# Linear attention on one core: K and V in 8 KB rows over eight heads, K's features written twice, a first matmul 128 wide

## The chip, the cores and the metric

The kernel runs on one core of a Trainium2 chip. A core has five engines with an instruction queue each: TensorE (PE, matrix products; PEld is its loading of weights), VectorE (DVE), ScalarE (ACT), GpSimd (POOL) and SyncE (SP). Each engine takes its instructions in the order in which the program gives them, and waits where one needs a result of another engine. Sixteen DMA engines move data between the chip's memory (DRAM) and the on-chip memory (SBUF, 128 partitions); POOL and SP issue the transfers here. PE writes to a second on-chip memory, PSUM, of eight banks. The metric is the device time of one execution in microseconds (us); lower is better.

## The reference

For every batch and head (8 x 12 of them, 512 rows of 64 elements, all f32) the kernel computes attention without a softmax, by way of a 64 x 64 matrix per head:

```python
Q_feat = np.maximum(0, Q) + 1
K_feat = np.maximum(0, K) + 1
KV = np.einsum('bhkd,bhkv->bhdv', K_feat, V)
K_sum = np.sum(K_feat, axis=2)
numerator = np.einsum('bhqd,bhdv->bhqv', Q_feat, KV)
denominator = np.einsum('bhqd,bhd->bhq', Q_feat, K_sum)
return numerator / (denominator[:, :, :, None] + 1e-10)
```

## The kernel before

The 49,152 rows of Q, K and V are cut into 6 steps of 16 heads. One transfer loads 2 MB of one input and writes it as 1 MB of bf16 (the cast is done on the way, by transfers that POOL issues); a step needs one each of K, V and Q. The output leaves as f32 in 12 transfers of 1 MB.

A **group** g (12 of them, two to a step) has eight heads. K and V lie in rows of 16 x 64 elements to a partition (4 KB in DRAM, `C2 = 16`), so a head fills 32 partitions, and four heads share a tile; a group takes two such tiles, n = 0 and 1. Q lies in rows of 32 x 64 elements (8 KB), so a head of Q fills 16 partitions.

For each group the program has these parts:

- `k_features` (L141): two DVE instructions of 1024 elements (L137) compute max(K + 1, 1), the same as max(0, K) + 1, for n = 0 and 1 into `kf`.
- `v_blocks` (L148): V is copied into `v_all`, a constant tile whose 32-partition blocks are a block diagonal: block b of the partitions fills columns 64b to 64b + 63 of 256, the rest stays zero, and 4 more columns hold ones for the sum over K's features. Three of the four blocks are copied by DVE (L155), one by ACT (L153). `clear` (L237) writes the zeros and ones once, at the start.
- `keys_values` (L166): the first product. For 16 values of c and n = 0, 1 a matmul with K's features as weights (128 partitions, 64 columns) and `v_all` as the moving operand (260 columns). The matmuls for n = 0 write PSUM partitions 0 to 63, those for n = 1 write 64 to 127. Four casts by ACT (L181, L182) put the result into `kva_diag`, as blocks on a diagonal.
- `q_features` (L159) and `transposes` (L184): Q's features by DVE, then 16 transposes on PE into two banks and two copies by ACT (L195) into `qt`.
- `output`: `out_matmuls` (L197), the second product, 32 matmuls with `qt` as weights (64 columns) and 130 moving columns; and `norms` (L214), four times a reciprocal of the denominator (L222) and a multiply (L223) from PSUM into `o_sb`, on DVE. A product of 8 matmuls fills two banks, and there are two such pairs, so PE runs at most two ahead of the norms.
- `load`, `load_q` and `store` (L96, L110, L122) issue the transfers. All loads but the first K, and all stores but the last two groups', are issued by POOL in one queue. `in_pool` has two buffers for each of K, V and Q, so the loads of step s + 2 wait for the copies of step s.

The order on each engine is written out by hand (`manual_schedule`, L247 on). A group's turn is: K's features, V copies, then `output` of the group two before, then transposes or Q features, then `keys_values` of this group. So on PE the output matmuls of an earlier group stand ahead of this group's first product. The last two groups have an order of their own (L282 to L299).

Of the kernel before, what the change touches and what calls it, by code (L numbers as in the profile page):

```python
# [9 lines left out]
BF16 = mybir.dt.bfloat16  # L10
ALU = mybir.AluOpType

BANK = 512
IN_BUFS = 2
OUT_BUFS = 3
LAG = 3
# [3 lines left out]
def kernel(  # L20
# [10 lines left out]

# [4 lines left out]
    C = 8  # L44
    C2 = 2 * C
    C4 = 4 * C
    R = 4
    NPAIR = B * H * S // (P * C)
    NP = 4
    NG = NPAIR // NP  # L50
# [5 lines left out]

    q_eights = view(Q, C4)
    k_dram = view(K, C2)
    v_dram = view(V, C2)
# [3 lines left out]
    head_pool = ctx.enter_context(tc.tile_pool(name="head_pool", bufs=1))  # L63
    in_pool = ctx.enter_context(tc.tile_pool(name="in_pool", bufs=IN_BUFS))
    kf_pool = ctx.enter_context(tc.tile_pool(name="kf_pool", bufs=2))
    qf_pool = ctx.enter_context(tc.tile_pool(name="qf_pool", bufs=3))
# [8 lines left out]
    NV = 4  # L75
    v_all = const.tile([P, 2, 2, C2, 4 * D1], BF16, name="v_all")
    ones = const.tile([P, 4], BF16, name="ones")
    zero = const.tile([P, 1], FP32, name="zero")
    kva_all = const.tile([P, NV, 4, 2, D1], BF16, name="kva_all")
    kva_diag = [kva_all[:, i] for i in range(NV)]  # L80

    drams = dict(k=k_dram, v=v_dram)
    raw = {}
    bufs = {}
# [4 lines left out]
    cells_of = {}  # L89

    def load_first_k():
        k_raw = head_pool.tile([P, 2, C2, D], FP32, name="k_first")
        nc.sync.dma_start(out=k_raw, in_=k_dram[:, 0:4:2])
        raw["k", 0] = k_raw

    def load(x, groups):  # L96
        s = groups[0] // 2
        if groups[0] % 2 == 0 or (x, s) not in bufs:
            bufs[x, s] = in_pool.tile([P, 4, C2, D], BF16, name=f"{x}_raw")
        if len(groups) == 2:  # L100
            ms = slice(0, 4)
            of = slice(4 * s, 4 * s + 4)
        else:
            ms = slice(groups[0] % 2, 4, 2)
            of = slice(4 * s + groups[0] % 2, 4 * s + 4, 2)
        nc.gpsimd.dma_start(out=bufs[x, s][:, ms], in_=drams[x][:, of])  # L106
        for g in groups:
            raw[x, g] = bufs[x, s][:, g % 2 : 4 : 2]

    def load_q(s):  # L110
        t = in_pool.tile([P, 2, C4, D], BF16, name="q_raw")
        nc.gpsimd.dma_start(out=t, in_=q_eights[:, 2 * s : 2 * s + 2])  # L112
        rows = t.rearrange("p n (r c) d -> p n r c d", c=C)
        for e in range(2):
            raw["q", 2 * s + e] = rows[:, :, :, 4 * e : 4 * e + 4]

    def load_pair(s):
        load("k", (2 * s, 2 * s + 1))
        load("v", (2 * s, 2 * s + 1))
        load_q(s)  # L120

    def store(g):  # L122
        s = g // 2
        o_to = o_dram[:, 2 * NP * s : 2 * NP * s + 2 * NP]
        if g < NG - 2:
            nc.gpsimd.dma_start(out=o_to[:, g % 2 : 2 * NP : 2], in_=outs[s][:, g % 2 : 2 * NP : 2])  # L126
            return
        if g == NG - 2:
            nc.sync.dma_start(out=o_to[:, 0 : 2 * NP : 2], in_=outs[s][:, 0 : 2 * NP : 2])
            return  # L130
        for h in range(2):
            nc.sync.dma_start(
                out=o_to[:, 2 * h + g % 2 : 2 * NP : NP], in_=outs[s][:, 2 * h + g % 2 : 2 * NP : NP]
            )

    def feature(dst, src):
        nc.vector.tensor_scalar(  # L137
            out=dst, in0=src, scalar1=1.0, scalar2=1.0, op0=ALU.add, op1=ALU.max
        )

    def k_features(g):  # L141
        k_raw = raw.pop(("k", g))
        kf = kf_pool.tile([P, C2, 2, D], BF16, name="kf")
        for n in range(2):
            feature(kf[:, :, n], k_raw[:, n])
        kfs[g] = kf

    def v_blocks(g):  # L148
        v_raw = raw.pop(("v", g))
        for b in range(4):  # L150
            ps = slice(32 * b, 32 * b + 32)
            if b == 3:
                nc.scalar.copy(out=v_all[ps, g % 2, :, :, b * D : b * D + D], in_=v_raw[ps])  # L153
            else:
                nc.vector.tensor_copy(  # L155
                    out=v_all[ps, g % 2, :, :, b * D : b * D + D], in_=v_raw[ps]
                )

    def q_features(g):  # L159
        q_raw = raw.pop(("q", g))  # L160
        qf = qf_pool.tile([P, R, C // 2, 2, D], BF16, name="qf")
        for n in range(2):
            feature(qf[:, :, :, n], q_raw[:, n])
        qfs[g] = qf

    def keys_values(g):  # L166
        kf = kfs.pop(g)
        kva_ps = psum_kva.tile([P, 4 * D1], FP32, name="kva_ps")
        for c in range(C2):
            for n in range(2):  # L170
                nc.tensor.matmul(  # L171
                    kva_ps[64 * n : 64 * n + 64],
                    lhsT=kf[:, c, n, :],
                    rhs=v_all[:, g % 2, n, c, :],
                    start=(c == 0),
                    stop=(c == C2 - 1),
                )
        kva = kva_diag[g % NV]
        for n in range(2):
            ps = slice(64 * n, 64 * n + 64)  # L180
            nc.scalar.copy(out=kva[ps, :, n, 0:D], in_=kva_ps[ps, 0 : 4 * D].rearrange("p (b d) -> p b d", b=4))  # L181
            nc.scalar.copy(out=kva[ps, :, n, D], in_=kva_ps[ps, 4 * D : 4 * D1])  # L182

    def transposes(g):  # L184
        qf = qfs.pop(g)
        if g % 2 == 0:
            qts[g // 2] = mid_pool.tile([P, C, P, R], BF16, name="qt")
        for half in range(2):
            qt_ps = psum_qt.tile([P, 2, R, P], BF16, name="qt_ps")
            for c in range(2):  # L190
                for r in range(R):
                    nc.tensor.transpose(qt_ps[:, c, r], qf[:, r, 2 * half + c, :, :], identity)  # L192
            copy = nc.vector.tensor_copy if half and g == NG - 2 else nc.scalar.copy
            lo = g % 2 * 4 + 2 * half
            copy(out=qts[g // 2][:, lo : lo + 2], in_=qt_ps.rearrange("p c r q -> p c q r"))  # L195

    def out_matmuls(g, h):  # L197
        qt = qts[g // 2]
        kva = kva_diag[(g // 2 * 2 + h) % NV]
        ops = [psum.tile([P, 2, BANK], FP32, tag="ps", name="o_ps") for _ in range(2)]  # L200
        for c in range(C):
            for j in range(2):
                b = 2 * (g % 2) + j
                q = 16 * (4 * h + b)
                nc.tensor.matmul(  # L205
                    ops[c // 4][64 * j : 64 * j + 64, c // 2 % 2, (c % 2) * W : (c % 2) * W + W],
                    lhsT=qt[:, c, q : q + 16, :],
                    rhs=kva[:, b],
                    start=True,
                    stop=True,  # L210
                )
        cells_of[g, h] = ops

    def norms(g, h):  # L214
        ops = cells_of.pop((g, h))
        if (g % 2, h) == (0, 0):
            outs[g // 2] = out_pool.tile([P, 2 * NP, C, D], FP32, name="o_sb")
        o_sb = outs[g // 2]
        for i in range(2):
            cells = ops[i][:, :, 0 : 2 * W].rearrange("p b (c n x) -> p b c n x", n=2, x=D1)  # L220
            recip = recip_pool.tile([P, 2, 2, 2, 1], FP32, name="recip")
            nc.vector.reciprocal(out=recip, in_=cells[:, :, :, :, D:D1])  # L222
            nc.vector.tensor_tensor(  # L223
                out=o_sb[:, 2 * h + g % 2 : 2 * NP : NP, 4 * i : 4 * i + 4].rearrange(
                    "p n (b c) d -> p b c n d", b=2
                ),
                in0=cells[:, :, :, :, 0:D],
                in1=recip.to_broadcast([P, 2, 2, 2, D]),
                op=ALU.mult,
            )  # L230

    def output(g):
        for h in range(2):
            out_matmuls(g, h)
            norms(g, h)

    def clear(i):  # L237
        t = v_all[:, i].rearrange("p n c x -> p (n c x)").bitcast(FP32)
        w = t.shape[1] * 5 // 8
        nc.vector.memset(t[:, 0:w], 0.0)  # L240
        nc.scalar.copy(out=t[:, w:], in_=zero.to_broadcast([P, t.shape[1] - w]))  # L241
        nc.vector.tensor_copy(
            out=v_all[:, i, :, :, 4 * D : 4 * D1].rearrange("p n c j -> p (n c) j"),
            in_=ones[:, None, :].to_broadcast([P, 2 * C2, 4]),
        )

    with tc.manual_schedule():  # L247
        nc.vector.memset(zero, 0.0)
        load_first_k()
        load("v", (0,))  # L250
        load_q(0)
        load("k", (1,))
        load("v", (1,))
# [11 lines left out]
        for g in range(last - 1):  # L265
            if g % 2:
                transposes(g - 1)
# [64 lines left out]
```

## Time and profile before

| | |
|---|---|
| median of 3 runs | 126.66 us (126.54 to 127.17) |
| span of the profiled execution, first to last instruction | 124.7 us |
| mean granted clock of TensorE | 0.847 of full |
| read from and written to DRAM | 37.75 MB and 12.58 MB, 404 GB/s over the span |
| shares of the chain that ended last | DMA 56%, DVE 19%, PE 8%, ACT 6% |
| DMA from issue to landing, median of 1 MB loads of K, V, Q | 22.1, 23.0, 26.0 us |

The profile is one execution, recorded by the hardware. Busy time is the time in which an engine had an instruction running; an engine's idle time is put down to what ended it (the releaser, behind the arrow <-). The chain that ended last is followed back from the last instruction, at each step to what released it. GB/s count what is written, so a load that turns f32 into bf16 counts half of what it reads. From issue to landing a load takes four to five times as long as its own share of the traffic, since other transfers stand ahead of it in the queue.

### The profile page before, as it was taken

How to read it: one execution, taken by the hardware profiler on the slowest of the kernel's cores; microseconds unless marked ns; L12 is line 12 of the kernel's file. 1: busy time of each engine (PE TensorE's matmuls, PEld its weight loads, DVE VectorE, ACT ScalarE, POOL GpSimd, SP SyncE). 2: the span in 40 equal slices, each digit the busy share in tenths (PEclk: the TensorE clock that was granted, in tenths of full speed). 3: DMA queues.
4: the chain of work that ended last, by engine and by line, in shares of the span. 5: the costliest groups of instructions: out<-in, count | busy, mean ns of one | idle time of the engine just before them, and what ended most of it. 6: DMA issues, size and time to landing. Idle time of an engine off the chain costs nothing.

```text
span 124.7 us, 2348 instructions
## 1 busy us (share of the span) xinstructions
PE 61.8 (50%) x960; PEld 50.7 (41%) x960; DVE 89.3 (72%) x191; ACT 59.6 (48%) x86; POOL 26.1 (21%) x51
## 2 busy tenths in 40 slices
PE   0004945200692838539684691069495267775300
PEld 0003735200581827428573490058384155663100
DVE  4895444206999899997999930699959699969700
ACT  7532289306039781956639462601993295450000
POOL 6991023100011630233302420302020200020000
PEclk9999999955589999995999689756999958997555
DMA  3999999999999999999999999999999999999993
GB/s 95 330 214 214 209 198 210 210 214 213 208 213 213 216 214 208 212 213 217 230 405 327 210 212 214 215 338 403 227 212 215 218 255 415 420 413 416 406 409 126
DMA packets 11803, 32.13 MB, mean 258 GB/s; under 512 B 528, under 2 KB 528, under 8 KB 11792
## 3 DMA queue, kind: packets, MB, share of 16 engines
q0 software_dynamic: 10448, 28.84, 97.4%
q1 hardware_dynamic: 1344, 3.15, 6.7%
q8 instruction: 7, 0.11, 0.3%
q14 instruction: 4, 0.03, 0.1%
HBM read 37.75 MB, written 12.58 MB: 404 GB/s over the span
## 4 chain that ended last, share of the span: by engine, by line
DMA 56%; DVE 19%; PE 8%; ACT 6%; issue 3%; POOL 2%; POOLq 0%
DMA v_raw<-in_V_dram 30%; DMA q_raw<-in_Q_dram 26%; DVE o_sb L223 8%; PE kva_ps L171 5%; DVE v_all L155 5%; ACT v_all L153 3%; DVE qf L137 2%; PE qt_ps L192 2%; DVE recip L222 2%; ACT qt L195 2%; POOL v_raw L106 1%; DVE qt L195 1%; ACT kva_all L181 1%; POOL k_raw L106 1%; DVE kf L137 1%
## 5 line engine op out<-in xcount | busy, mean ns | idle before, releaser
L205 PE MATMUL o_ps<-kva_all,qt 128*64 128x130 bf16 x384 | 20.0, 240 | 37.0 <-DVE recip L222 27.0
L171 PE MATMUL kva_ps<-v_all,kf 128*64 128x260 bf16 x384 | 29.8, 320 | 15.8 <-DVE v_all L155 15.6
L155 DVE COPY v_all<-v_raw 32x2048 bf16<-32x2048 bf16 x36 | 25.8, 717 | 13.5 <-DMA v_raw<-in_V_dram 13.1
L223 DVE TENSOR_TENSOR o_sb<-o_ps,recip 128x512 f32<-128x512 f32 x48 | 33.2, 692 | 1.6
L171 PEld LDWEIGHTS <-kf 128*64 128x64 bf16 x384 | 24.6, 130 | 19.0 <-DVE v_all L155 16.0
L205 PEld LDWEIGHTS <-qt 128*64 128x64 bf16 x384 | 14.0, 118 | 42.2 <-issue 26.0
L153 ACT COPY v_all<-v_raw 32x2048 bf16<-32x2048 bf16 x12 | 22.6, 1893 | 16.9 <-DMA v_raw<-in_V_dram 16.7
L195 ACT COPY qt<-qt_ps 128x1024 bf16<-128x1024 bf16 x23 | 22.2, 1015 | 6.8 <-PE qt_ps L192 6.5
L181 ACT CAST kva_all<-kva_ps 64x256 bf16<-64x256 f32 x24 | 8.9, 371 | 27.5 <-PE kva_ps L171 27.3
L126 POOL DMA_DIRECT2D out_dram<-o_sb x10 | 8.6, 864 | 35.9 <-DVE o_sb L223 27.2
L192 PE MATMUL qt_ps<-identity,qf 128*128 128x128 bf16 x192 | 14.8, 235 | 2.0 <-ACT qt L195 1.3
L192 PEld LDWEIGHTS <-qf 128*128 128x128 bf16 x192 | 12.4, 106 | 4.5 <-issue 2.5
L137 DVE TENSOR_SCALAR kf<-k_raw 128x1024 bf16<-128x1024 bf16 x22 | 8.5, 426 | 7.6 <-DMA k_raw<-in_K_dram 7.6
L106 POOL DMA_DIRECT2D k_raw<-in_K_dram x6 | 4.9, 822 | 35.0 <-DVE kf L137 35.0
L222 DVE RECIPROCAL recip<-o_ps 128x8 f32<-128x8 f32 x48 | 9.6, 200 | 1.4 <-PE o_ps L205 1.2
L137 DVE TENSOR_SCALAR qf<-q_raw 128x1024 bf16<-128x1024 bf16 x24 | 8.8, 431 | 2.1 <-DMA q_raw<-in_Q_dram 2.0
L106 POOL DMA_DIRECT2D v_raw<-in_V_dram x7 | 5.4, 766 | 13.4 <-ACT v_all L153 9.3
L240 DVE MEMSET v_all<- 128x2600 f32 x2 | 4.5, 2225 | 0.9 <-issue 0.9
L112 POOL DMA_DIRECT2D q_raw<-in_Q_dram x6 | 4.3, 716 | 0.0
L182 ACT CAST kva_all<-kva_ps 64x4 bf16<-64x4 f32 x24 | 4.1, 170 | 0.0
L241 ACT COPY v_all<-zero 128x1560 f32<-128x1560 f32 x2 | 2.9, 1487 | 0.0
L261 POOL MEMSET kva_all<- 128x130 bf16 x16 | 2.4, 201 | 0.0
(13 smaller groups left out, 5.8 us busy)
## 6 DMA issues: line engine op xcount, KB each, us to landing
out_dram<-o_sb POOLq DMA_DIRECT2D x10, 1024.0 KB, 25.7
q_raw<-in_Q_dram POOLq DMA_DIRECT2D x6, 1024.0 KB, 26.0
k_raw<-in_K_dram POOLq DMA_DIRECT2D x5, 1024.0 KB, 22.1
v_raw<-in_V_dram POOLq DMA_DIRECT2D x5, 1024.0 KB, 23.0
k_first<-in_K_dram SPq DMA_DIRECT2D x1, 1024.0 KB, 4.9
v_raw<-in_V_dram POOLq DMA_DIRECT2D x2, 512.0 KB, 10.7
out_dram<-o_sb SPq DMA_DIRECT2D x1, 1024.0 KB, 7.0
out_dram<-o_sb SPq DMA_DIRECT2D x2, 512.0 KB, 6.4
```

The costliest lines, as they stand in the source:

```text
L106: nc.gpsimd.dma_start(out=bufs[x, s][:, ms], in_=drams[x][:, of])
L126: nc.gpsimd.dma_start(out=o_to[:, g % 2 : 2 * NP : 2], in_=outs[s][:, g % 2 : 2 * NP : 2])
L137: nc.vector.tensor_scalar(out=dst, in0=src, scalar1=1.0, scalar2=1.0, op0=ALU.add, op1=ALU.max)
L153: nc.scalar.copy(out=v_all[ps, g % 2, :, :, b * D : b * D + D], in_=v_raw[ps])
L155: nc.vector.tensor_copy(out=v_all[ps, g % 2, :, :, b * D : b * D + D], in_=v_raw[ps])
L171: nc.tensor.matmul(kva_ps[64 * n : 64 * n + 64], lhsT=kf[:, c, n, :], rhs=v_all[:, g % 2, n, c, :], start=(c == 0), stop=(c == C2 - 1),)
L181: nc.scalar.copy(out=kva[ps, :, n, 0:D], in_=kva_ps[ps, 0 : 4 * D].rearrange("p (b d) -> p b d", b=4))
L192: nc.tensor.transpose(qt_ps[:, c, r], qf[:, r, 2 * half + c, :, :], identity)
L195: copy(out=qts[g // 2][:, lo : lo + 2], in_=qt_ps.rearrange("p c r q -> p c q r"))
L205: nc.tensor.matmul(ops[c // 4][64 * j : 64 * j + 64, c // 2 % 2, (c % 2) * W : (c % 2) * W + W], lhsT=qt[:, c, q : q + 16, :], rhs=kva[:, ...
L222: nc.vector.reciprocal(out=recip, in_=cells[:, :, :, :, D:D1])
L223: nc.vector.tensor_tensor(out=o_sb[:, 2 * h + g % 2 : 2 * NP : NP, 4 * i : 4 * i + 4].rearrange("p n (b c) d -> p b c n d", b=2), in0=cell ...
```

## The change

K and V are now loaded in rows of 32 x 64 elements (8 KB), as Q is. A head fills 16 partitions, a tile holds eight heads, and a step s (`NPAIR` = 6) has two tiles, n = 0 and 1, each the work of one group before.

With two heads in each block of 32 partitions, the block diagonal of V alone no longer keeps them apart. K's features are therefore written twice, for a = 0 and 1, with the partitions of the other head at zero: instead of the constants 1 and 1 the instruction takes two values per partition from memory, `shift` and `least`, that make either max(K + 1, 1) or max(K + lowest, 0) = 0. `masks` computes them once, from bit 4 of the partition number. The two versions lie beside each other in `kf`, so that the first product is one matmul with 128 columns of weights per c, 32 of them per tile, in place of 2 x 16 with 64.

The stores write the same rows as before (2 KB), 12 of 1 MB; the last is no longer cut in two. `o_sb` is now six tiles of 1 MB in place of three of 2 MB, and the first K is loaded into one of them.

The order by hand is another one: in each half of a step `keys_values` now comes ahead of `output` of the step before, the transposes of a step stand at its end, and the last steps have no order of their own. The diff, cut to its core:

```diff
-    C2 = 2 * C
+    ROWS = 32
-    q_eights = view(Q, C4)
-    k_dram = view(K, C2)
-    v_dram = view(V, C2)
+    q_dram = view(Q, ROWS)
+    k_dram = view(K, ROWS)
+    v_dram = view(V, ROWS)
...
+    lane = const.tile([P, 1], I32, name="lane")
+    odd = const.tile([P, 1], I32, name="odd")
+    least = const.tile([P, 2], FP32, name="least")
+    shift = const.tile([P, 2], FP32, name="shift")
+    v_alls = [const.tile([P, ROWS, 4 * D1], BF16, name=f"v_all{i}") for i in range(2)]
+    kvas = [const.tile([P, 8, 2, D1], BF16, name=f"kva{i}") for i in range(2)]
...
+    def k_features(s, n):
+        k_raw = raw.pop(("k", s, n))
+        kf = kf_pool.tile([P, ROWS, 2, D], BF16, name="kf")
+        for a in range(2):
+            nc.vector.tensor_scalar(
+                out=kf[:, :, a],
+                in0=k_raw,
+                scalar1=shift[:, a : a + 1],
+                scalar2=least[:, a : a + 1],
+                op0=ALU.add,
+                op1=ALU.max,
             )
...
-        for c in range(C2):
-            for n in range(2):
-                nc.tensor.matmul(
-                    kva_ps[64 * n : 64 * n + 64],
-                    lhsT=kf[:, c, n, :],
-                    rhs=v_all[:, g % 2, n, c, :],
-                    start=(c == 0),
-                    stop=(c == C2 - 1),
-                )
+        for c in range(ROWS):
+            nc.tensor.matmul(
+                kva_ps,
+                lhsT=kf[:, c].rearrange("p a d -> p (a d)"),
+                rhs=v_alls[n][:, c],
+                start=(c == 0),
+                stop=(c == ROWS - 1),
+            )
+        kva = kvas[s % 2]
+        po = slice(64 * n, 64 * n + 64)
+        for a in range(2):
+            pi = slice(64 * a, 64 * a + 64)
+            nc.scalar.copy(
+                out=kva[po, a::2, n, 0:D],
+                in_=kva_ps[pi, 0 : 4 * D].rearrange("p (b d) -> p b d", b=4),
+            )
+            nc.scalar.copy(out=kva[po, a::2, n, D], in_=kva_ps[pi, 4 * D :])
...
+    def masks():
+        nc.vector.tensor_scalar(out=odd, in0=lane, scalar1=16, scalar2=None, op0=ALU.bitwise_and)
+        nc.vector.tensor_scalar(
+            out=least[:, 0:1], in0=odd, scalar1=-1.0 / 16, scalar2=1.0, op0=ALU.mult, op1=ALU.add
+        )
+        nc.vector.tensor_scalar(
+            out=least[:, 1:2], in0=odd, scalar1=1.0 / 16, scalar2=None, op0=ALU.mult
+        )
+        nc.vector.tensor_scalar(
+            out=shift, in0=least, scalar1=-1.0, scalar2=-LOWEST, op0=ALU.add, op1=ALU.mult
+        )
+        nc.vector.tensor_tensor(out=shift, in0=shift, in1=least, op=ALU.add)
...
+        nc.gpsimd.iota(lane, pattern=[[0, 1]], base=0, channel_multiplier=1)
...
         clear(0)
+        masks()
...
+        for s in range(NPAIR):
+            k_features(s, 0)
+            v_blocks(s, 0)
+            keys_values(s, 0)
+            if s:
+                output(s - 1, 0)
+                if s > 1:
+                    store(s - 2, 1, nc.gpsimd)
+            k_features(s, 1)
+            v_blocks(s, 1)
+            q_features(s)
+            keys_values(s, 1)
+            if s:
+                output(s - 1, 1)
+            if s + 2 < NPAIR:
+                load_k(s + 2)
+                load_v(s + 2)
+                load_q(s + 2)
+            if s:
+                store(s - 1, 0, nc.gpsimd)
+            transposes(s, 0)
+            transposes(s, 1)
+        s = NPAIR - 1
+        store(s - 1, 1, nc.gpsimd)
+        output(s, 0)
+        store(s, 0, nc.sync)
+        output(s, 1)
+        store(s, 1, nc.sync)
```

## The prediction

> **What bounds the kernel now.** I read the page first: which engine is busy when. Columns of its first line are busy us, share of the span and instructions; the strips cut the span into 40 slices, busy share in tenths and GB/s moved.
>
> ```profile
> PE 61.8 (50%) x960; PEld 50.7 (41%) x960; DVE 89.3 (72%) x191; ACT 59.6 (48%) x86; POOL 26.1 (21%) x51
> ...
> DMA  3999999999999999999999999999999999999993
> GB/s 95 330 214 214 209 198 210 210 214 213 208 213 213 216 214 208 212 213 217 230 405 327 210 212 214 215 338 403 227 212 215 218 255 415 420 413 416 406 409 126
> ...
> q0 software_dynamic: 10448, 28.84, 97.4%
> ```
>
> The 16 DMA engines are full from the second slice to the last, whatever computes. A load writes bf16 at about 213 GB/s (1.049 MB in 4.9 us), a store f32 at about 415 (1.049 MB in 2.5 us). Eighteen loads' worth (the first K in f32 at 2.5 us, the rest 85.8 us) and 12 stores (30 us) make 118 us of a 124.7 us span. The kernel is bound by DMA; no engine's own work reaches 90 us.
>
> Second, the groups by line with shapes kept apart, for prices (last columns: busy us, mean ns of one; idle us before the group and what ended it).
>
> ```profile
> L223 DVE TENSOR_TENSOR o_sb<-o_ps,recip 128x512 f32<-128x512 f32 x48 | 33.2, 692 | 1.6
> L171 PE MATMUL kva_ps<-v_all,kf 128*64 128x260 bf16 x384 | 29.8, 320 | 15.8 <-DVE v_all L155 15.6 <-ACT v_all L153 0.2
> L155 DVE COPY v_all<-v_raw 32x2048 bf16<-32x2048 bf16 x36 | 25.8, 717 | 13.5 <-DMA v_raw<-in_V_dram 13.1
> ...
> L153 ACT COPY v_all<-v_raw 32x2048 bf16<-32x2048 bf16 x12 | 22.6, 1893 | 16.9 <-DMA v_raw<-in_V_dram 16.7
> L195 ACT COPY qt<-qt_ps 128x1024 bf16<-128x1024 bf16 x23 | 22.2, 1015 | 6.8 <-PE qt_ps L192 6.5
> ...
> L137 DVE TENSOR_SCALAR kf<-k_raw 128x1024 bf16<-128x1024 bf16 x22 | 8.5, 426 | 7.6 <-DMA k_raw<-in_K_dram 7.6
> ...
> L137 DVE TENSOR_SCALAR kf<-k_first 128x1024 bf16<-128x1024 f32 x2 | 1.5, 782 | 0.0
> ```
>
> VectorE (DVE) waits for almost nothing but DMA. That is due to the order on PE: ahead of each step's first product stand the output matmuls of two steps before, whose inputs are long ready, so the norms follow the V copies without a wait.
>
> Third, the timeline (start, us taken by the run of instructions, engine, line), for runs of matmuls:
>
> ```profile
> 48.04 1.96 PE L171 MATMUL kva_ps<-v_all,kf 128*64 128x260 bf16 x32
> ...
> 50.14 1.07 PE L192 MATMUL qt_ps<-identity,qf 128*128 128x128 bf16 x16
> ...
> 51.14 0.64 PE L205 MATMUL o_ps<-kva_all,qt 128*64 128x130 bf16 x16
> ...
> 100.97 3.24 PE L171 MATMUL kva_ps<-v_all,kf 128*64 128x260 bf16 x32 [2.69 <-DVE v_all L155]
> ...
> 107.92 1.93 ACT L195 COPY qt<-qt_ps 128x1024 bf16<-128x1024 bf16 x2 [1.69 <-PE qt_ps L192]
> ...
> 108.58 1.98 PE L171 MATMUL kva_ps<-v_all,kf 128*64 128x260 bf16 x32
> ...
> 110.83 0.21 DVE L222 RECIPROCAL recip<-o_ps 128x8 f32<-128x8 f32 x1 [1.16 <-PE o_ps L205]
> ```
>
> A product (32 matmuls of the first kind) takes 1.98 us at its best (62 ns each) and more after an idle PE: 3.24 at 100.97, 3.68 for the run at 11.12, where the clock is low. The twelve sum to 29.8 us, 2.48 each. The last line shows what the change will make the rule: DVE waiting while a product ahead of its output matmuls runs.
>
> **The change part by part.** Nothing changes in number or shape for V copies (48), Q features (24), transposes (192), output matmuls (384), norms (48 reciprocals, 48 multiplies), casts of the product (48) and stores (12 MB). What changes:
>
> *Rows of 8 KB.* The end-of-transfer packets of the trace lie 4.89 to 4.92 us apart for the Q loads, whose rows are 8 KB already, and 4.95 to 5.60 for the ten 1 MB loads of K and V, 51.2 us in sum. All at 4.90 saves 2.2 us, at the least row 0.5. It counts only while DMA is the bound.
>
> *K's features twice.* 24 instructions stay 24, of 2048 elements in place of 1024, with a scalar from memory in place of constants. No row has such a scalar. Lower bound: the bf16 copy of 2048 elements, 0.69 us from one start to the next, 1.38 a pair (now 0.76). Upper: the multiply with two inputs, 512 in 0.692 us, so 5.5 a pair. I take 1.38, since operation, element type and output pitch are those of line 137, which at 1024 runs at about the copy's rate. The first pair reads f32: 1.48 us for 2 x 1024, so about 2.8 for 2 x 2048. A page bears on this: the Trainium skill, "PSUM — Partial Sum Buffer", section "Specifications (TRN2)", says that a [P, 1] operand passed as a scalar does not count among the inputs that decide whether VectorE takes two elements at a time; by that the pair is 1.38 and the first rival below falls, but no row here shows it.
>
> *Masks.* Five small DVE operations behind the first clear, between the 0.06 us of a small memset and the 0.20 of a reciprocal: 0.3 to 1.0, I take 0.6. Their iota on POOL (0.1 to 0.3, as its memset and select rows) stands behind four load issues and is done by about 4.6, when the clear is. First K features so start at 8.1, not 7.4.
>
> *First matmul 128 wide.* As many instructions (384), but the two 64-wide ones for two heads, which used separate halves of the array, become one over the whole array. Lower bound: 1.98 us a product, if width costs nothing. Upper: twice the slowest row, 7.4. Near rows: 16 transposes, 128 wide, 128 columns, take 1.07 us (67 ns); 16 output matmuls, 64 wide, 130 columns, 0.64 (40 ns). Halves of the array do run side by side, so I double: 3.96 at full clock, 4.97 at the mean (2 x 2.48), and 5.7 for the first, cold one (3.7 us of warming at twice 115 ns, the rest at 124). PE will have idle stretches of 3 to 5 us ahead of every product, so I take 4.97 for all others. A rule: the Trainium skill, "TensorE: Matmul & The Clock Gate", section "Back-to-back issue gap", gives 260/2.4 + 2.5 = 111 ns warm and 217 cold, so 3.55 and 6.9 us a product; all warm the sum below would be an estimated 159 us, and started cold for the 3.4 us that its section "What's actually happening" names, 5.2 each and 178.
>
> *The order, which decides.* On PE the product of a step now stands ahead of the output matmuls of the step before, and DVE has norms next behind the V copies. So DVE stands still through each product from the second step on, 10 times. Behind the waiting reciprocal wait the next K features and V copies, and for those the next product waits. Transposes stand at a step's end, their four copies on ACT ahead of ACT's share of the next V.
>
> One step, from the start of the four norms of an output's second half (0):
> - norms 3.45 (0.84 apart), K pair 1.38, V copies 2.15: DVE done at 6.98.
> - PE: last output matmuls at 2.1 (bank freed by the second norm), transposes 0.55 per 8; ACT's four copies (0.97 each, two banks) end at 6.5, ACT's V copy 1.89: 8.4.
> - product 8.5 to 13.4, first 8 output matmuls 0.27: norms at 13.7, then K pair and V copies: 20.7.
> - product again (Q features, 1.43, hidden in it) and 0.27: 26.0.
>
> A step is 26.0 us, where DMA needs 14.7 (three loads) or 19.7 (and two stores). So loads land long before they are wanted, and DMA's full strip goes.
>
> Start: K features 8.1 to 10.9, V to 13.0, product to 18.8, casts 0.95, ACT's V copy (it stands behind them) to 21.6, product to 26.6, casts 27.5, four copies 31.4, ACT's V copy 33.3 (V landed at 29.1, so DMA is no limit), product and 0.27 to 38.7, 6.98 to 45.7, product and 0.27 to 50.9. Four steps more: 50.9 + 4 x 26.0 = 154.8. The end: transposes and copies to 161.3, second norm of the last pair of outputs at 161.7, seven norms from there, 6.0, to 167.7. The last store, now 1 MB in one on SP's queue, lands 4.9 us on (the first K's row, an idle queue), and the span ends 0.9 later, as now: 173.5. The shown median is 2.0 above this execution's span (126.66 against 124.7), so 175.5 us.
>
> If the cover of these waits came back (output matmuls ahead of the product) the step would fall to DVE's 15.1 us of work and DMA would bound again.
>
> **The rivals.**
> - *Scalars from memory are slow.* For it: the f32 row (782 ns for 1024) shows that DVE has slower rates. Against: nothing but the scalar differs. Pair at 3.0 us (f32 rate) gives the same sum 184; at 5.5, 208.
> - *Width is free.* Products stay at 1.98 to 2.48, as if 62 ns were an instruction's cost. Against: output matmuls issue every 40 ns. Sum 143 to 148: still slower, by the order alone.
> - *The clock stays low*: products at 7.4, 204 us. Against: 1.98 rows directly after other PE work.
> - *The other side: DMA still sets the end.* If DVE's waits fit into what DMA leaves, the time is the present one less the 0.5 to 2.2 us of the rows: 124.4 to 126.2. It decides once a step takes under 19.7 us; 26.0 less two products (2 x 4.97) is 16.0, so each product would have to appear for at most 1.8 us. For it: DVE has 28% idle now. Against: program order on PE.
>
> **How the numbers follow.** Forecast (products 3.6 to 5.4, fast scalars) 0.72: 159 to 180. Slow scalars 0.14. Width free 0.07. Low clock 0.04. DMA bound 0.03. The likeliest is 175 us. The range 152 to 192 leaves out free width, the DMA bound, the slower half of slow scalars and low clock: about 0.2. Under 0.5% is no change that a measurement here can tell; of the last case's 0.03, 0.02 are faster by more and 0.01 within it; slower 0.97.
>
> **What would show it.** Right: DVE's reciprocals wait some 10.5 us a step for the output matmuls (6.7 and 3.8), about 50 in all; DMA share near 0.7 with gaps; product runs of 4 to 5.4 us; K features 0.7 us each; steps 26 us apart. Wrong: DMA strip full to the end, products near 2 us, K features over 1 us, or DVE's waits on DMA as now.

## The result, and the profile after

The changed kernel takes 182.66 us (median of 4 runs, 181.13 to 182.94), the kernel before in the same runs 126.62 us: a ratio of 1.4386, 95% interval 1.4326 to 1.4447. The profiled execution took 182.94 us with a span of 181.2 us. The prediction was 175 us, with a range of 152 to 192.

First the page of the changed kernel: which engine is busy when, in the same columns and strips as before, then the shares of the chain that ended last.

```profile
PE 98.6 (54%) x960; PEld 71.8 (40%) x960; DVE 97.9 (54%) x195; ACT 60.0 (33%) x87; POOL 24.4 (13%) x52
...
PE   0019394581686392495392395293395293395550
...
DVE  6883734019619309809409909408909508907680
...
PEclk9999879579579879579879579879579879579955
DMA  5999999999999990599992499992600600600666
...
q0 software_dynamic: 7504, 28.84, 67.2%
...
PE 42%; DVE 33%; ACT 19%; issue 2%; ACTq 1%; DVEq 0%
```

DMA's strip, full to the end before, has holes from the 16th slice on, and the queue that carries the loads and most stores is at work for 67% of the span in place of 97%. No engine is busy for more than 55%. The strips of PE and DVE are the thing to look at: where one shows 9 the other shows little. They work in turn, and the chain that ended last goes from PE to DVE to ACT and back without a DMA in it.

Second, the groups: busy us and mean ns of one, then the idle time ahead of the group and what ended it.

```profile
L144 PE MATMUL kva_ps<-v_all,kf 128*128 128x260 bf16 x384 | 66.9, 355 | 55.8 <-DVE v_all L125 37.1 <-ACT v_all L123 18.7
...
L192 DVE RECIPROCAL recip<-o_ps 128x8 f32<-128x8 f32 x48 | 9.6, 200 | 65.0 <-PE o_ps L183 65.0
...
L107 DVE TENSOR_SCALAR kf<-k_raw,shift,least 128x2048 bf16<-128x2048 bf16 x22 | 17.4, 834 | 4.1 <-DMA k_raw<-in_K_dram 4.1
```

The product has gone from 29.8 to 66.9 us, and PE waits 37.1 us for the V copies of DVE and 18.7 us for those of ACT, six times each. DVE's reciprocals, which waited 1.2 us for output matmuls before, wait 65.0 us. PE and DVE stand still for each other: 37.1 us here, 65.0 us there.

Third, the timeline of one step of the changed kernel (start, us, engine, line; in brackets the idle time ahead and what ended it).

```profile
67.84 0.21 DVE L192 RECIPROCAL recip<-o_ps 128x8 f32<-128x8 f32 x1 [7.35 <-PE o_ps L183]
...
71.20 1.53 DVE L107 TENSOR_SCALAR kf<-k_raw,shift,least 128x2048 bf16<-128x2048 bf16 x2
72.65 2.27 DVE L125 COPY v_all<-v_raw 32x2048 bf16<-32x2048 bf16 x3
...
74.98 5.75 PE L144 MATMUL kva_ps<-v_all,kf 128*128 128x260 bf16 x32 [4.90 <-DVE v_all L125]
...
81.12 0.21 DVE L192 RECIPROCAL recip<-o_ps 128x8 f32<-128x8 f32 x1 [4.68 <-PE o_ps L183]
...
83.95 3.76 ACT L171 COPY qt<-qt_ps 128x1024 bf16<-128x1024 bf16 x4 [2.29 <-PE qt_ps L170]
...
86.04 2.06 DVE L125 COPY v_all<-v_raw 32x2048 bf16<-32x2048 bf16 x3
...
87.74 1.89 ACT L123 COPY v_all<-v_raw 32x2048 bf16<-32x2048 bf16 x1
...
89.68 5.23 PE L144 MATMUL kva_ps<-v_all,kf 128*128 128x260 bf16 x32 [3.14 <-ACT v_all L123]
...
95.30 0.21 DVE L192 RECIPROCAL recip<-o_ps 128x8 f32<-128x8 f32 x1 [7.20 <-PE o_ps L183]
```

It reads as a closed circle: the V copies end at 74.9, the product runs to 80.7, only then come the output matmuls that DVE's next norms need (81.12), behind these norms stand the next K features and V copies, and behind those the next product. This next product (89.68) waits longer for another engine: DVE has done its V copies at 88.1, but ACT's V copy stands behind the four copies of the transposes and ends at 89.6. The four norms of an output's second half come again 27.6 us after those at 53.50, then after 27.4, 27.3 and 27.3 us.

Every product has an idle PE ahead of it. What that does is in a view of PE and its granted clock (PEclk) during the product that starts at 74.98: us of the stretch, busy time and matmuls in it, clock, and then DMA share and GB/s, which play no part here.

```profile
75.00:76.00 1.00, 1.00 (x5) 0.50 0.77 106
76.00:77.00 1.00, 1.00 (x7) 0.50 1.01 201
77.00:78.00 1.00, 1.00 (x7) 0.50 1.01 201
78.00:79.00 1.00, 1.00 (x6) 0.50 1.04 209
79.00:80.00 1.00, 1.00 (x10) 0.93 1.11 225
```

For 4 us the clock stays at half, and a matmul starts every 216 ns; then it is full, and one starts every 112 ns. The Trainium skill, "TensorE: Matmul & The Clock Gate", section "Back-to-back issue gap", gives figures that the trace agrees with: 217 and 111 ns at 260 columns.

### The profile page after: what moved, and what is told of

Read it like the earlier page. It is cut to its first block, busy times and chain, and to the rows that moved or that the text cites. A ratio compares the mean times of both kernels' runs of the same rounds, so it can differ in the third digit from the quotient of the medians.

```text
span 181.2 us, 2346 instructions
## 1 busy us (share of the span) xinstructions
PE 98.6 (54%) x960; PEld 71.8 (40%) x960; DVE 97.9 (54%) x195; ACT 60.0 (33%) x87; POOL 24.4 (13%) x52
## 4 chain that ended last, share of the span: by engine, by line
PE 42%; DVE 33%; ACT 19%; issue 2%; ACTq 1%; DVEq 0%
PE kva_ps L144 37%; DVE o_sb L193 14%; ACT qt L171 12%; DVE v_all L125 7%; ACT v_all L123 6%; DVE kf L107 5%; PE o_ps L183 3%; DVE recip L192 3%; DVE v_all L218 2%; PE qt_ps L170 2%; ACT kva L155 1%; ACTq L298 1%; DVE v_all L220 0%; ACT kva L159 0%; DVE shift L210 0%
## 5 line engine op out<-in xcount | busy, mean ns | idle before, releaser
L144 PE MATMUL kva_ps<-v_all,kf 128*128 128x260 bf16 x384 | 66.9, 355 | 55.8 <-DVE v_all L125 37.1
L144 PEld LDWEIGHTS <-kf 128*128 128x128 bf16 x384 | 47.9, 126 | 73.4 <-DVE v_all L125 46.5
L155 ACT CAST kva<-kva_ps 64x256 bf16<-64x256 f32 x24 | 8.9, 372 | 93.9 <-PE kva_ps L144 93.8
L183 PE MATMUL o_ps<-kva,qt 128*64 128x130 bf16 x384 | 19.2, 232 | 14.4 <-DVE o_sb L193 10.2
L183 PEld LDWEIGHTS <-qt 128*64 128x64 bf16 x384 | 12.7, 113 | 21.4 <-DVE o_sb L193 14.1
L107 DVE TENSOR_SCALAR kf<-k_raw,shift,least 128x2048 bf16<-128x2048 bf16 x22 | 17.4, 834 | 4.1 <-DMA k_raw<-in_K_dram 4.1
L170 PE MATMUL qt_ps<-identity,qf 128*128 128x128 bf16 x192 | 13.7, 219 | 6.2 <-ACT qt L171 6.2
L170 PEld LDWEIGHTS <-qf 128*128 128x128 bf16 x192 | 11.3, 97 | 8.2 <-issue 7.7
L159 ACT CAST kva<-kva_ps 64x4 bf16<-64x4 f32 x24 | 4.0, 168 | 0.0
L107 DVE TENSOR_SCALAR kf<-o_sb,shift,least 128x2048 bf16<-128x2048 f32 x2 | 2.6, 1340 | 0.0
## 6 DMA issues: line engine op xcount, KB each, us to landing
q_raw<-in_Q_dram POOLq DMA_DIRECT2D x6, 1024.0 KB, 16.1
```

The source lines that it names most:

```text
L107: nc.vector.tensor_scalar(out=kf[:, :, a], in0=k_raw, scalar1=shift[:, a : a + 1], scalar2=least[:, a : a + 1], op0=ALU.add, op1=ALU.max,)
L144: nc.tensor.matmul(kva_ps, lhsT=kf[:, c].rearrange("p a d -> p (a d)"), rhs=v_alls[n][:, c], start=(c == 0), stop=(c == ROWS - 1),)
L155: nc.scalar.copy(out=kva[po, a::2, n, 0:D], in_=kva_ps[pi, 0 : 4 * D].rearrange("p (b d) -> p b d", b=4),)
L170: nc.tensor.transpose(qt_ps[:, c, r], qf[:, r, lo + c], identity)
L183: nc.tensor.matmul(o_ps[64 * t : 64 * t + 64, c // 2, (c % 2) * W : (c % 2) * W + W], lhsT=qt[:, 4 * i + c, 16 * k : 16 * k + 16], rhs=kva ...
```

## The experiments

Three explanations of the 56 us were to be told apart: the order on PE (the product ahead of ready output matmuls), the width of the product's matmuls, and the low clock after each idle stretch; beside them the scalars from memory and what the new layout itself costs or brings. All kernels were compared with the kernel before on the same chip (126.58 to 126.79 us). In the kernels with narrow products half of the first product is left out, and `const_scalars` masks no head, so these are probes and no replacements.

**The order alone.** In the kernel before, `keys_values` is moved ahead of `output`:

```diff
+            keys_values(g)
             ...
-            keys_values(g)
```

> The kernel before with one thing done: in its main loop keys_values stands ahead of output, as the change has it; 4 KB rows, 64-wide products and the hand-made order of the last two groups stay. Theory (the order alone already ends the DMA bound): VectorE waits for a product of 2.0 to 3.7 us in each of ten groups, a step of two groups takes 20 to 22 us against 14.7 to 19.7 for DMA, and the time is 132 to 146 us. Rival (order is harmless while products are 64 wide): 125 to 128.

152.53 us, ratio 1.2039 (1.1986 to 1.2092): 26 us slower, more than the 132 to 146 expected. The timeline of this kernel shows one of its half steps:

```profile
58.85 0.21 DVE L222 RECIPROCAL recip<-o_ps 128x8 f32<-128x8 f32 x1 [4.13 <-PE o_ps L205]
...
64.23 2.32 DVE L155 COPY v_all<-v_raw 32x2048 bf16<-32x2048 bf16 x3
...
68.00 3.68 PE L171 MATMUL kva_ps<-v_all,kf 128*64 128x260 bf16 x32 [3.08 <-ACT v_all L153]
...
72.14 0.21 DVE L222 RECIPROCAL recip<-o_ps 128x8 f32<-128x8 f32 x1 [5.58 <-PE o_ps L205]
```

It is the changed kernel's circle with the old matmuls. What had been missed in the expectation is the product's length: 3.32 to 3.68 us in eleven of twelve, where the kernel before has seven at 1.96 to 1.98. The wait does not only add the product to the path, it also makes the product long.

**The same, with PE kept busy.** 30 matmuls of the identity on itself, ahead of each product of that kernel:

```diff
+        for _ in range(30):
+            nc.tensor.matmul(kva_ps[:, 0:P], lhsT=identity, rhs=identity, start=True, stop=True)
```

> The kernel before with keys_values ahead of output (as in products_first) and 30 matmuls of the identity on PE ahead of each product, their result overwritten. It parts the wait that the order makes from the low clock that the wait brings. Theory (the order costs twice: VectorE waits for each product, and PE, standing still meanwhile, starts each product at half clock): products of 2.0 to 2.4 us in place of 3.3 to 3.7, ten of them on the path, and 134 to 141 us in place of 152.5. Rival (64-wide products were slow for another reason than PE's standing still): products stay above 3.2 and the time at 150 to 156.

142.48 us, ratio 1.124 (1.1188 to 1.1292), a little above the expected. The first three products still take 3.24 to 3.36 us; from the fourth on, they take 1.98 to 2.33. So of the order's 26 us at least 10 (152.53 to 142.48) are the low clock that the wait brings with it, and at most 16 the wait.

**The order undone in the changed kernel**: `output` ahead of `keys_values` in both halves of a step.

```diff
-            keys_values(s, 0)
             if s:
                 output(s - 1, 0)
                 ...
+            keys_values(s, 0)
```

> The changed kernel with one thing undone: in both halves of a step the output matmuls and norms of the step before stand ahead of keys_values again, everything else as it is. Theory (the order makes VectorE wait): VectorE no longer waits for products; what is left per step is 15.5 us of its own work and a wait of some 4 us for the four copies of the transposes, so a step is about 19.6 in place of 27.6, and the time 140 to 150 us. Rival (the 128-wide products bound the kernel wherever they stand, 67 us of them and cold): above 170.

141.27 us, ratio 1.115 (1.1085 to 1.1215): 41 us are gone by the order, nothing else being touched. Seven of the twelve products take 3.74 or 3.75 us, which is the warm price, and DVE's waits for output matmuls fall from 65.0 to 23.3 us, as the view of waits of this kernel says (total, times, longest):

```profile
DVE recip L192 <- PE o_ps L183: 23.3, 13, 6.4
```

**The width undone in the changed kernel.** The 32 matmuls of a product become 64 wide, alternately for a = 0 and 1:

```diff
+            a = c % 2
             nc.tensor.matmul(
-                kva_ps,
-                lhsT=kf[:, c].rearrange("p a d -> p (a d)"),
+                kva_ps[64 * a : 64 * a + 64],
+                lhsT=kf[:, c, a, :],
                 rhs=v_alls[n][:, c],
-                start=(c == 0),
-                stop=(c == ROWS - 1),
+                start=(c < 2),
+                stop=(c >= ROWS - 2),
```

> The changed kernel with 64-wide products in alternate halves of the array: as many matmuls (32 a product), half of the columns of weights each, so half of the first product is left out. Order and everything else stay. Theory (width doubles the price of a wait that the order makes): a cold 64-wide matmul takes 108 ns, a warm one 56 (from the starts in the trace of before), so products of about 3.2 to 3.6 us in place of 5.6, 12 on the path: 154 to 162 us. Rival (64 or 128 columns cost the same): 181 to 183.

159.92 us, ratio 1.2622 (1.2417 to 1.2827). All twelve products are cold, 3.57 to 3.68 us: narrower matmuls on the same path are still on the path. In the timeline of this kernel:

```profile
65.55 3.66 PE L145 MATMUL kva_ps<-v_all,kf 128*64 128x260 bf16 x32 [4.90 <-DVE v_all L125]
...
69.48 0.21 DVE L193 RECIPROCAL recip<-o_ps 128x8 f32<-128x8 f32 x1 [2.47 <-PE o_ps L184]
```

The idle time of PE is the 4.90 us of the changed kernel, and DVE's wait is 2.47 in place of 4.68 us.

**PE kept busy in the changed kernel**, order and width as they are: 24 or 44 identity matmuls ahead of each product, which run while PE would wait.

```diff
+        for _ in range(44 if n else 24):
+            nc.tensor.matmul(kva_ps[:, 0:P], lhsT=identity, rhs=identity, start=True, stop=True)
```

> The changed kernel with 24 (first half) and 44 (second half) matmuls of the identity with itself put on PE ahead of each product, in time in which PE now stands still; their result is overwritten. Theory (the clock: each product starts at about 216 ns a matmul and gets to 112 after 12 to 22 of them, because PE stood still for 3 to 5 us before it): products of 3.6 to 4.2 us, and 12 x 1.4 to 2.0 less, 159 to 166 us. Rival (the slow first matmuls come from 128-wide weights or from PSUM, not from standing still): products stay at 5.0 to 6.1, 182 to 190 us.

164.01 and 167.44 us in two runs, where 159 to 166 was expected. More matmuls, and 15 to 19 us less: the product now has its warm price, ten times at 3.74 or 3.75 us. The timeline of this kernel:

```profile
63.31 2.63 PE L144 MATMUL kva_ps<-identity 128*128 128x128 bf16 x44
...
68.28 3.75 PE L146 MATMUL kva_ps<-v_all,kf 128*128 128x260 bf16 x32 [2.34 <-DVE v_all L125]
...
72.42 0.21 DVE L194 RECIPROCAL recip<-o_ps 128x8 f32<-128x8 f32 x1 [2.69 <-PE o_ps L185]
```

The product that took 5.75 us takes 3.75, and DVE's wait falls by as much (4.68 to 2.69). All twelve products of this kernel sum to 48.0 us, 18.9 less than the changed kernel's 66.9, and 15 to 19 of that show in the time.

**Order and width undone together.** The two edits from above in one kernel.

> Both earlier edits at once: output ahead of keys_values, and 64-wide products in alternate halves of the array (half of the first product left out). Theory (width costs only as far as a product is on the path): products 2.0 to 3.7 us, and 4 to 11 us less than the 141.3 of the order alone, 130 to 137 us, where the same edit took 23 us from the changed kernel. Rival (width costs the same in either order): about 118 to 122.

135.12 us, ratio 1.0666 (1.0631 to 1.0701). With the order undone the width costs 6 us (141.27 to 135.12); in the change's order it costs 23 (182.66 to 159.92). The groups of the two kernels with the order undone, wide first:

```profile
L144 PE MATMUL kva_ps<-v_all,kf 128*128 128x260 bf16 x384 | 54.7, 310 | 16.9 <-DVE v_all L125 12.8 <-ACT v_all L123 4.0
...
L145 PE MATMUL kva_ps<-v_all,kf 128*64 128x260 bf16 x384 | 38.7, 385 | 16.9 <-DVE v_all L125 16.4 <-ACT v_all L123 0.5
```

In the change's order the products fall by 22.9 us (66.9 to 44.0), and all of it shows in the time. Here they fall by only 16.0, since eleven of the twelve narrow ones take 2.79 to 3.68 us in place of the 1.96 of a warm one; and of the 16.0 only 6 show, about as much as DVE's waits for output matmuls fall by (23.3 to 16.1 us). So two things make the width cheaper in this order.

**The scalars.** Constants in place of `shift` and `least`:

```diff
-                scalar1=shift[:, a : a + 1],
-                scalar2=least[:, a : a + 1],
+                scalar1=1.0,
+                scalar2=1.0,
```

> The changed kernel with the constants 1 and 1 in place of the two scalars from memory, so that both versions of K's features are the same and no head is masked. Theory (scalars from memory cost little): a pair takes about 1.4 in place of 1.5 to 1.6 us, and the 11 pairs on the path save 1 to 2 us: 180 to 182. Rival (the scalar takes VectorE out of its fast rate): K features fall by a third or more and the time to 175 or less.

182.75 us, ratio 1.4425 (1.4394 to 1.4457): no gain. Yet the instructions are shorter, in the groups of this kernel:

```profile
L107 DVE TENSOR_SCALAR kf<-k_raw 128x2048 bf16<-128x2048 bf16 x22 | 14.2, 686 | 4.3 <-DMA k_raw<-in_K_dram 4.3
```

834 less 686 is 0.15 us for each, and a pair takes 1.20 us from its start to the V copies in place of 1.44 to 1.55. Only the pairs ahead of the six products that wait last for DVE are on the path; the expectation counted eleven. That makes some 1.7 us in all. Where it goes is seen in the products:

```profile
74.75 5.93 PE L144 MATMUL kva_ps<-v_all,kf 128*128 128x260 bf16 x32 [4.66 <-DVE v_all L125]
...
81.07 0.21 DVE L192 RECIPROCAL recip<-o_ps 128x8 f32<-128x8 f32 x1 [4.87 <-PE o_ps L183]
```

The product starts 0.23 us earlier than the changed kernel's (74.98) and takes 0.18 us longer (5.93 against 5.75), so DVE's next norms start 0.05 us earlier, at 81.07. The granted clock rose at 79.1 us in the one kernel and at 79.3 in the other, and what was won ahead of that was spent on more matmuls at half the clock. Ahead of the last two of the six products, DVE's V copies besides took 2.27 us in place of 2.06.

**Can the layout reach the time before?** First, the outputs of a half step are put half a step later and ahead of the product, so that DVE need not wait for a product that has just run; the last two steps have an order of their own, with 20 identity matmuls ahead of a product, and the last store is cut in two. The core of it:

```diff
         for s in range(last):
             k_features(s, 0)
             v_blocks(s, 0)
+            if s > 1:
+                output(s - 2, 1)
+                store(s - 2, 1, nc.gpsimd)
             keys_values(s, 0)
             k_features(s, 1)
             v_blocks(s, 1)
             q_features(s)
+            if s:
+                output(s - 1, 0)
             keys_values(s, 1)
```

> The changed kernel (8 KB rows, K's features twice, 128-wide products) with another order: each output half a step later than in the change and ahead of the product on PE, so that its inputs have long been ready; in the last step the norms of the step before fill the waits, 20 idle matmuls warm PE ahead of the last two products, and the last store is cut in two. Theory (order and not the wider work made it slow; DMA binds again, and rows of 8 KB load 0.05 to 0.7 us faster per MB): 124 to 127 us. Rival (15.5 us of VectorE's work a step and 7.5 of products are too much for DMA's 14.7 to 19.7 us): 130 or more.

136.56 us, ratio 1.0775 (1.0696 to 1.0854), a miss. The loads are about as early as in the kernel before (the last Q lands at 104.35 us, before at 103.72); the time is lost behind them, in the last two steps. Its timeline:

```profile
91.57 3.74 PE L146 MATMUL kva_ps<-v_all,kf 128*128 128x260 bf16 x32
...
95.15 1.05 PE L172 MATMUL qt_ps<-identity,qf 128*128 128x128 bf16 x16
...
98.78 0.65 PE L184 MATMUL o_ps<-kva,qt 128*64 128x130 bf16 x16
...
99.24 0.21 DVE L200 RECIPROCAL recip<-o_ps 128x8 f32<-128x8 f32 x1 [5.00 <-PE o_ps L184]
...
110.09 7.89 PE L146 MATMUL kva_ps<-v_all,kf 128*128 128x260 bf16 x64
...
118.38 0.21 DVE L200 RECIPROCAL recip<-o_ps 128x8 f32<-128x8 f32 x1 [3.53 <-PE o_ps L184]
```

DVE waits 5.00 us, from 94.24 on, for an output behind a product and the transposes of step 4. The product ends at 95.3 and so makes 1.1 of the 5.00; the rest is the transposes, which wait for ACT's copies. It waits 3.53 us for an output behind the last two products, which run one after the other.

Second, these two places are mended: one output is drawn ahead, and the last product is put behind the norms of the step before.

```diff
+            if s == last - 1:
+                output(s - 1, 1)
+                store(s - 1, 1, nc.gpsimd)
...
-        output(s - 2, 1)
-        store(s - 2, 1, nc.gpsimd)
...
-        keys_values(s, 1)
...
+        keys_values(s, 1)
```

> half_step_later with the last steps in another order: the second output of step 3 moved ahead of the transposes of step 4, and the first norms of step 4's second output ahead of the last product. Theory (what half_step_later lost to DMA was VectorE waiting 5.0 and 3.5 us in the last two steps): 131 to 134 us. Rival (VectorE's work alone, 98 us in place of 89, keeps it behind): no better than 136.

132.22 and 134.68 us in two runs, where 131 to 134 was expected; 5.5 to 8.0 us above the kernel before (126.70) remain. A guess for them was DVE's longer work, 98.7 us busy against 89.3. So third, of `tail_reordered`, one of DVE's V copies went to ACT:

```diff
-            if b == 3:
+            if b >= 2:
                 nc.scalar.copy(out=dst, in_=v_raw[ps])
```

> tail_reordered with two of V's four blocks copied by ScalarE in place of one: 8.5 us of copies leave VectorE, 22.7 come to ScalarE. Theory (with the order mended, the 9 us that the second writing of K's features adds to VectorE are what is left): 126 to 130 us. Rival (ScalarE's copies now hold up the products): slower than tail_reordered.

162.20 us, ratio 1.2765 (1.2664 to 1.2866): a clear miss. DVE's work fell to 89.7 us, and that was worth nothing, since a copy takes 1.9 us on ACT against 0.7 on DVE. The groups of this kernel:

```profile
L146 PE MATMUL kva_ps<-v_all,kf 128*128 128x260 bf16 x384 | 61.5, 335 | 38.2 <-ACT v_all L123 26.0
...
L123 ACT COPY v_all<-v_raw 32x2048 bf16<-32x2048 bf16 x24 | 45.5, 1896 | 3.8 <-DMA v_raw<-in_V_dram 3.2
```

The products now wait for ACT, 26.0 us in sum, find PE at half clock again and take 5.2 to 5.4 us in the steady steps.

Fourth and fifth, the guess itself was tried on `tail_reordered`: with the 64 wide product alone (the edit of half_width), and with that and K's features written once (`range(1)` in place of `range(2)`).

> The kernel tail_reordered with matmuls of the first product that are 64 wide, alternately for the two copies of K's features (half of the first product is left out). It asks what of the 6.8 us that tail_reordered stays behind the kernel before is the width. Theory A, the products in the last steps (DVE waits of 1.45, 3.27, 0.87 and 0.25 us for output matmuls, and the first 12.8 us wait before the first product): 127 to 130 us. Theory B, DVE's own work (98.7 us busy against 89.3, of which 10.0 us are K's features at 2048 elements): no gain by width, 132 to 134 us.

> As tail_half_width, and K's features written once only, for a = 0 (24 fewer-by-half instructions on DVE: 12 of 2048 elements, and the product reads that copy alone; half of K's features and half of the first product are left out). DVE's busy time falls to about 88.7 us, as in the kernel before, and the layout's loads and stores stay. Theory A: about the time of tail_half_width, within 1 us. Theory B: 4 to 7 us below it, and so 126 to 128 us. If it stays above 129 us, neither width nor features make the rest, and the layout's order of transfers or the tail does.

127.12 us, ratio 1.0023 (1.0003 to 1.0044), and 126.90 us, ratio 1.002 (0.9995 to 1.0045). With narrow products the whole rest is gone. DVE's extra work is then worth nothing that can be told: busy 98.6 us in the one and 89.5 in the other. Both are bound by DMA, though, and wide products with K's features written once were not tried, so it is not shown that this work costs nothing beside wide products. The last chain and the DMA strip of `tail_half_width`:

```profile
DMA  4999999999999999999999999999999999999795
...
DMA 49%; DVE 30%; ACT 5%; issue 5%; PE 4%; POOL 1%; ACTq 1%; POOLq 0%
```

and the strip of `tail_reordered`, in whose last chain no DMA stands:

```profile
DMA  3999999999999999999999999999999999923695
```

Without the width DMA is the bound again. In `tail_reordered` the last two products take 4.51 and 3.75 us, in `tail_half_width` 1.96 and 1.94. DVE's wait for an output behind them is 3.27 us in the first:

```profile
116.13 0.21 DVE L200 RECIPROCAL recip<-o_ps 128x8 f32<-128x8 f32 x1 [3.27 <-PE o_ps L184]
```

and 0.35 us in the second:

```profile
110.75 0.21 DVE L201 RECIPROCAL recip<-o_ps 128x8 f32<-128x8 f32 x1 [0.35 <-PE o_ps L185]
```

No version beat the kernel before. The 8 KB rows were not tried by themselves.

## Why the prediction was right, and where its sizes were off

- **The order decides: right.** It was forecast as ten products on DVE's path; the reciprocals waited eleven times, 65.0 us, where "about 50" was said. Ten of the waits are for outputs behind a product, and the eleventh, 2.36 us, is in the end. Undoing the order alone takes 41 us off.
- **A step of 26.0 us: 27.3 to 27.6.** From the norms at 53.50 (forecast 50.9) to those at 163.08 (forecast 154.8) four steps lost 5.7 us, and the start 2.6; the end, 18.1 us from there to the span's end, was forecast at 18.7.
- **Inside the range, but above its main part.** The 159 to 180 us that were given 0.72 stood for products of 3.6 to 5.4 us, and the time is 182.66, with products of 5.58. The room above 180 had been made for slow scalars (184 us), which did not come. That the range still holds the time is in part luck; the mechanism is not.
- **The term that was mis-sized: "I take 4.97 for all others".** The products take 5.58 us in the mean. The price of a warm matmul was set too high (124 ns for 112) and that of a cold one too (230 for 216), but the mean of the kernel before, which was doubled, is one of seven warm products and five cold or mixed ones. In the new order none is warm from the start: each begins at half clock and stays there for 2.6 to 4.9 us, 3.8 in the mean (for the first this is read from its matmuls' starts, 216 ns apart, as the trace has no clock record before 17.7 us). The prediction had seen the idle stretches of 3 to 5 us, and took the old mean all the same. Two products of a steady step are 5.75 + 5.23 = 10.98 for 9.94: 1.0 of the 1.4 us that a step is longer. The estimate by the Trainium skill, "TensorE: Matmul & The Clock Gate", section "What's actually happening", 3.4 us at half clock and so 5.2 each and 178 us, was the nearer one; it too was short of the 3.8 us measured.
- **K's pair: 1.38, measured 1.44 to 1.55** from its start to the V copies. The fast rate was kept, as was taken; the scalars add 0.15 us to an instruction (834 against 686 ns). With products of 5.55 and pairs of 1.5 the prediction's own sum gives 182.5. That slow scalars would decide (184 to 208) falls by `const_scalars`: without them the time is the same. The Trainium skill, "PSUM — Partial Sum Buffer", section "Specifications (TRN2)", has it that such a scalar does not count for the pairing of elements. The trace agrees as far as the rate goes: 834 ns for 2048 elements is far from the twice 686 that a halved rate would take.
- **Masks and first clear: right.** The five small operations lie between 4.34 and 5.24 us (0.90 where 0.6 was taken), the first K features start at 8.17 (forecast 8.1).
- **Width is free: no.** A warm product of 32 wide matmuls takes 3.74 us, one of 32 narrow ones 1.96: the doubling held.
- **DMA still sets the end: no.** That DMA would bind again with the output matmuls ahead of the product came true only in part. In `out_first`, with just that, the time is 141.27 us, DVE still waits 23.3 us for output matmuls, and no DMA stands in the last chain. In `tail_half_width`, with ready outputs ahead of the product and narrow matmuls, DMA is the bound again, at 127.12 us. The 1.8 us that a product may appear for was not tried by itself.
- **Rows of 8 KB, 0.5 to 2.2 us where DMA binds: not seen.** The first loads of K and V land 4.89 and 4.90 us apart, where they took 5.31 and 5.60, but in `half_step_later` the last Q landed at 104.35 us for 103.72; and `tail_half_width`, bound by DMA, is not faster than the kernel before.

So the 56 us are, in one order of taking them apart, 26 for the order alone (at least 10 of them the low clock that it brings) and 30 for the rest on top of it. Of these 23 come back with narrow matmuls; the other 7 were not taken apart.

## What to carry to other kernels

On engines that take their work in order, a long product ahead of ready work for another engine turns a pipeline into a circle: ask of each instruction what stands behind it, and who waits for that. Such a wait has a second price, since the waiting PE loses its clock: a product's price is to be taken from rows with the same idle time and as little work ahead of them, not from a mean over rows of another schedule. And the same edit (here 64 or 128 columns) costs 6 or 23 us, depending on whether its instructions stand on the path and on the clock that they find.

## What the runs showed of the hardware that was not expected

- An instruction that starts earlier need not end earlier: in `const_scalars` the product at 74.75 began 0.23 us sooner and the clock rose when it would have risen anyway, so the matmuls in between ran at half rate and most of what DVE had saved was lost. In the trace of the changed kernel the clock changes only after 3.41, 6.83 or 10.24 us, multiples of 3.41, and it keeps to multiples of 3.41 us in the traces of all other runs too.
- A pause is not the only thing that costs the clock; little work does too. In `tail_half_width` a product starts at 47.44 with no idle time ahead of it, right behind output matmuls, and takes 3.61 us. The view of PE and its clock in this kernel:

```profile
43.60:47.40 3.80, 1.60 (x40) 1.00 1.07 216
47.40:49.00 1.60, 1.60 (x24) 0.51 1.04 210
```

PE was at work for 1.60 of the 3.80 us ahead of it, in pieces with a longest pause of 1.88 us, and the clock fell to half just as the product began. `tail_reordered` does the same work at that place with a wide product, which finds the full clock and takes 3.74 us. So narrow products may take about as long as wide ones: four of the six from 36.96 to 83.06 us take 3.3 to 3.6 us. The last two, the first of them right behind identity matmuls, are at their best.
- In the changed kernel the pauses of 3.14 and 4.90 us ahead of a product were each long enough for half clock; in `kept_busy` pauses of 1.80 and 2.23 to 2.34 us, behind 24 or 44 identity matmuls in a row, were not. But one pause there of 2.35 us was:

```profile
42.64 5.41 PE L146 MATMUL kva_ps<-v_all,kf 128*128 128x260 bf16 x32 [2.35 <-DVE v_all L125]
```

The pause alone does not decide it. If all traces here are cut at the multiples of 3.41 us at which their clock changes, the clock stayed full after windows in which PE was busy for 0.42 of the time or more (236 windows), halved after windows with 0.60 or less (97), and came back after windows with 0.77 or more (97). Between 0.42 and 0.60 both happened, so this share is not the whole rule. The window with the pause ahead of 42.64 has 0.31, the one ahead of the narrow product at 47.44 has 0.35. A warm narrow product fills 0.57 of a window (1.96 us), a wide one more than the whole (3.74), which fits that narrow products lose the clock more easily; no run varies this share alone.
